# A two-layer diffusion step on one core: when weight tiles are split, and where modulation steps stand in a tile

## The chip, the core and the metric

The kernel runs on one core of a Trainium2 chip. The metric is the device time of one launch in microseconds. The engines named below are TensorE (PE, with its weight loads as PEld), VectorE (DVE), ScalarE (ACT), GpSimd (POOL) and SyncE (SP, which here only issues transfers). Each engine runs its own instructions strictly in the order of the program, and waits at an instruction until what it needs is there.

## What is computed

Two groups of rows (512 rows of a sample, 128 of a prompt, 640 in all) go through the same two layers. Cut to what matters:

```python
sh1, sc1, ga1, sh2, sc2, ga2 = split(silu(c) @ w_ada[l] + b_ada[l], 6)   # modulation
h = rmsnorm(x) * (1 + sc1) + sh1
z = h @ w_in[l]              # q, k, v | gq, gk, gv, gate, gate ranks
o_na  = attention(q, k, v)   # sample: window and cached keys; prompt: all keys
o_gla = gated_linear_attention(gq, gk, gv, forget gates), both directions
x = x + ga1 * (concat(o_na, rmsnorm(o_gla) * silu(gate)) @ w_o[l])
x = x + ga2 * (relu((rmsnorm(x) * (1 + sc2) + sh2) @ w_up[l]) ** 2 @ w_down[l])
```

All matrices are 1024 wide, the hidden layer of the MLP 4096. Everything is to be had at the accuracy of fp32.

## The kernel before

Activations lie transposed: 8 blocks of 128 features by 640 rows. A weight tile is 128x1024 (512 KB). A **split** makes two tiles of it: `wh`, a rounded copy (ACT), and `wl`, what the rounding lost (POOL, or DVE at the start of the program). A block of activations is split likewise, and a product is the sum of three: `wh` by the high part, `wh` by the low part, `wl` by the high part (`mm3`). A tile of the projection (`proj`) takes eight such groups, one for each block `kc`, six matrix products each, and then an evacuation from PSUM.

Weights come through three stages in `prefetch`: a transfer from SP's queue into a raw buffer `wr` (three of them), the split into a pair `wh`, `wl` (three pairs), and the use. `used`, called at the end of a tile, sets its pair free and calls `prefetch`, which at once writes down the split of a further tile, ahead of the evacuation of the tile that has just ended. So two tiles are ready when a tile begins, and the third is split while that tile runs.

The **modulation steps** (`ada_step`) work out `silu(c) @ w_ada` for all of layer 1 and most of layer 0, a 128x1024 tile of `w_ada` at a time, on DVE: two `scalar_tensor_tensor` instructions, one for each condition (`cbc`), each with an accumulated sum. In layer 0's attention half there is one step for each of the projection's tiles 6 to 23, and some more in the output projection. There `adab` is 1, and the raw tile of a step takes one of the same three `wr` buffers; in the MLP half (`adab` is 2) the steps have buffers of their own (`ar`). With `adab` 1 a step is written down after the evacuation of its tile.

Between the weight products PE takes the small products of attention, written as generators (`gla_pair`, `gv_task`, `qk_task`, `na_unit`) which a planner (`Drv`, with times estimated by `Est`) slips in between the groups of a tile. PE's order is fixed by that. The order on the other engines is set by a list scheduler, by priority and estimated time: `high_priority(offset=650)` in `prefetch` puts splits and transfers ahead of what was written before them. A dependency of class `NoSync` binds that order alone: no wait is put into the program for it.

Names in the traces: `ks`, `ksT` are decayed keys and their transposed copy, `ST` (in layer 1 `cbc`) the states, `ex` decay factors, `PN`, `tot` their sums, `A`, `Dg` the score blocks, `row` an activation block (here also a head's output), `sqo` its square, `gt`, `V`, `gv` values, `sq`, `sqh`, `sql` squares for the QK-norm, `gg` the output gate, `junk` a place for results that nobody reads. Every instruction carries line 197, that of a helper that records it, so groups go by names.

Of the kernel before, what the change touches and what calls it, by code (L numbers as in the profile page):

```python
# [211 lines left out]
class Kern:  # L212
# [13 lines left out]
    def run(self):  # L226
# [43 lines left out]
        self.wprep = self.wused = self.nada = 0  # L270
        self.adap, self.adab = None, 1
        self.wx = None
        self.raw, self.hl, self.over = {}, {}, set()
        self.rot, self.nacc = False, 0
        with self.pool("start") as sp, self.pool("norm_s", 2) as npl:
# [142 lines left out]
        for _ in range(self.steps_at(*key)):  # L418
            self.ada_step(*self.steps.pop(0))

    def prefetch(self, ahead=650):
        nc = self.nc
        with self.tc.high_priority(offset=ahead):
            go = True
            while go:
                go = False
                i = self.nld
                if i < min(len(self.units), self.npos + self.DEPTH, self.ldmax):
# [26 lines left out]
                    elif len(self.raw) + (self.nada if self.adab == 1 else 0) < self.NRAW:  # L455
# [2 lines left out]
                        self.raw[i] = t  # L458
                        self.nld += 1
                        go = True  # L460
                if self.raw and self.wprep - self.wused < (self.NHL if self.wx is None else self.NHL + 1):
                    j = min(self.raw)
                    wx = self.wx is not None and self.wprep == self.NHL
                    t = self.raw.pop(j)
                    if wx:
                        h, lo = (self.wx.tile([128, 1024], F32R, name=n) for n in ("wxh", "wxl"))
                    else:
                        h = self.wp.tile([128, 1024], F32R, name="wh", tag="wh", bufs=self.NHL)
                        lo = self.wp.tile([128, 1024], F32R, name="wl", tag="wl", bufs=self.NHL)
                    self.est.ready[t.name] = max(self.est.ready[t.name], self.dv.t)  # L470
                    nc.scalar.activation(out=h, in_=t, func=AF.Copy)
                    if self.wx is not None:
                        nc.vector.tensor_tensor(out=lo, in0=t, in1=h.bitcast(F32), op=ALU.subtract)
                    elif self.units[j] in self.units[max(0, j - 4):j] + self.units[j + 1:j + 5]:

                        nc.vector.tensor_tensor(out=lo[:, :448], in0=t[:, :448], in1=h[:, :448].bitcast(F32), op=ALU.subtract)
                        nc.gpsimd.tensor_tensor(out=lo[:, 448:], in0=t[:, 448:], in1=h[:, 448:].bitcast(F32), op=ALU.subtract)
                    else:
                        nc.gpsimd.tensor_tensor(out=lo, in0=t, in1=h.bitcast(F32), op=ALU.subtract)
                    self.hl[j] = (h, lo)  # L480
                    self.wprep += 1
                    go = True

    def unit(self, *key):
        i = self.ntake
# [15 lines left out]
    def ada_step(self, l, v, kc):  # L501


        nc = self.nc
        ui, t = self.unit("ada", l, v, kc)
        junk = self.junk()
        for r in range(2):
            i = nc.vector.scalar_tensor_tensor(out=junk if r == 0 else t, in0=t, scalar=1.0, in1=self.cbc[:, r], op0=ALU.mult,
                                           op1=ALU.mult, accum_out=self.mod[l][:, v, kc, r:r + 1])
            if self.adab == 1:  # L510

                self.tc.add_manual_dep(i.ins, self.lastmm.ins.name, mybir.DependencyInfo(
                    mybir.DependencyClass.NoSync, mybir.DependencyReason.DATA), reason="order")
        if kc == KC - 1:
            b0 = PC_BADA + 48 * l + 8 * v
            m = self.mod[l][:, v]
            nc.vector.tensor_tensor(out=m, in0=m, in1=self.pc[:, b0:b0 + KC, None].to_broadcast([128, KC, 2]), op=ALU.add)
        self.used(ui)
# [77 lines left out]
    def proj(self, key, evac):  # L596

        n = TX if self.lateh else T
        ui, w = self.unit(*key)
        wh, wl = (t.rearrange("p (k m) -> p k m", k=KC) for t in w)  # L600
        ps, nsm = self.acc_any(n=n)
        for kc in range(KC):
            self.mm3(ps, wh[:, kc], wl[:, kc], *self.h[kc], kc == 0, kc == KC - 1)
            if kc == 0 and self.adab > 1:
                self.ada_at(*key)
            if kc < KC - 1:
                yield
        self.used(ui)
        with self.tc.high_priority(offset=self.EVP):
            evac(ps[1])  # L610
        self.acc_done(ps, nsm)
        if self.adab == 1:
            self.ada_at(*key)
        yield

    def first_steps(self, keys):
# [250 lines left out]
    def layer(self, l):  # L867
# [11 lines left out]
        with self.pool(f"att{l}", reuse_waits="tile") as ap:  # L879
# [7 lines left out]
            with self.pool(f"gla{l}", reuse_waits="tile") as gp:  # L887
# [22 lines left out]
                    self.filler(self.z_tile(l, z_evac))  # L910
                else:
                    self.filler(self.first_b(l, [z_evac] + [lambda segs, i=i: self.gla_rope(l, 0, i, segs) for i in range(2)]))
                for h in range(2 if l == 0 else 0, 4):
                    dv.take("gt")
                    self.filler(self.proj(nxt(), lambda ps: self.start(self.gv_task(h, ps))))
# [17 lines left out]
            with self.pool(f"na{l}", reuse_waits="tile") as np_:  # L933
# [13 lines left out]
                for h in range(4):  # L947
                    hh, hl = self.pair_rows(ra, h)
                    nc.scalar.activation(out=hh, in_=self.gg[h], func=AF.Copy)
                    nc.gpsimd.tensor_tensor(out=hl, in0=self.gg[h], in1=hh.bitcast(F32), op=ALU.subtract)  # L950
                    self.aT[4 + h] = (hh, hl)
                x = [self.row(rb, kc, F32) for kc in range(KC)]
                for j in range(4):
                    for kc in range(2 * j, 2 * j + 2):
# [779 lines left out]
```

## Time and profile before

| | before |
|---|---|
| three runs, us | 1740.12, 1748.31, 1747.23 (median 1747.23) |
| profiled execution, its own time, us | 1745.39 |
| its span, us | 1743.6 |
| PE busy | 1653.4 us, 95% of the span |
| DVE, ACT, POOL busy | 62%, 40%, 36% |
| mean granted clock of TensorE | 0.979 |
| read from memory | 170.36 MB, 102 GB/s over the span |

The program has a start (0 to 60 us), the attention half of layer 0 (60 to 460: gated linear attention up to 260, then neighbourhood attention), the MLP half of layer 0 (460 to 880), the attention half of layer 1 (880 to 1300) and the MLP half of layer 1 (to the end). The page's line of 40 slices shows PE at 9 tenths or more in the MLP halves, and at 7 to 9 in the attention halves. A time in brackets in the rows is how long the engine stood idle ahead of the instruction, and the name behind it is what ended that. The granted clock is 1.00 at 2.4 GHz and 0.50 at 1.2 GHz.

### The profile page before, as it was taken

The numbers are of one execution on the slowest core, as the hardware profiler recorded it, in microseconds if no ns is written. First come the engines' busy times: TensorE is split into PE (matmuls) and PEld (weight loads), VectorE is DVE, ScalarE is ACT, GpSimd is POOL, SyncE is SP. The second block draws the span as 40 slices with busy tenths as digits, with TensorE's granted clock in tenths as the row PEclk, the third lists the DMA queues.
The fourth block names the chain that finished last, engine by engine and source line by source line (L and its number), as shares of the span: only waits on it lengthen the run. The fifth ranks groups of instructions, "written<-read, shape, count | busy, mean of one in ns | idle before, by whom it ended". The sixth has DMA issues, their size and how long they took to land. (4 is left out here: it accounts for less than half of the span.)

```text
span 1743.6 us, 32610 instructions
## 1 busy us (share of the span) xinstructions
PE 1653.4 (95%) x13712; PEld 1575.1 (90%) x13712; DVE 1076.4 (62%) x1971; ACT 703.3 (40%) x1142; POOL 626.7 (36%) x266
## 2 busy tenths in 40 slices
PE   7988788989999999999989899999999999999999
PEld 6977677779999999999988788888999999999998
DVE  5686767788797788777677737586662222222322
ACT  3535335543543233322344445466454223332330
POOL 1234432113334444444345536313233333333331
PEclk9998899999999999999999989999999999999999
DMA  9121233233354454445241111323222222222221
GB/s 369 45 65 64 92 105 119 77 110 121 121 181 139 157 166 134 144 147 169 76 168 51 51 43 57 91 69 94 70 65 84 73 73 73 74 83 74 73 73 73
DMA packets 61345, 179.28 MB, mean 103 GB/s; under 512 B 6928, under 2 KB 17808, under 8 KB 61200
## 3 DMA queue, kind: packets, MB, share of 16 engines
q1 hardware_dynamic: 45360, 159.76, 27.4%
q10 hardware_dynamic: 15840, 17.45, 3.2%
q8 instruction: 108, 1.77, 0.4%
q14 instruction: 37, 0.30, 0.1%
HBM read 170.36 MB, written 6.82 MB: 102 GB/s over the span
## 5 line engine op out<-in xcount | busy, mean ns | idle before, releaser
L197 POOL TENSOR_TENSOR wl<-wr,wh 128x1024 fp32r<-128x1024 f32 (+1 forms) x188 | 490.1, 2608 | 906.0 <-ACT wh L197 856.5
L197 PE MATMUL ps_mm<-row,wh 128*128 128x256 f32 (+1 forms) x2416 | 485.8, 322 | 7.9 <-DVE row L197 3.7
L197 ACT ACTIVATE wh<-wr 128x1024 fp32r<-128x1024 f32 x195 | 206.3, 1058 | 627.7 <-PE ps_sm L197 400.7
L197 PEld LDWEIGHTS ps_mm<-row,wh 128*128 128x128 f32 x2416 | 399.7, 193 | 30.3 <-issue 18.7
L197 PE MATMUL ps_mm<-row,wl 128*128 128x256 f32 (+2 forms) x1208 | 282.7, 313 | 0.5 <-DVE wl L197 0.5
L197 PEld LDWEIGHTS ps_mm<-row,wl 128*128 128x128 f32 x1208 | 224.8, 192 | 0.9 <-DVE wl L197 0.7
L197 DVE SCALAR_TENSOR_TENSOR row<-ps_sm,mod,row 128x256 f32<-128x256 f32 (+1 forms) x216 | 81.8, 432 | 97.0 <-PE ps_sm L197 97.0
L197 DVE SCALAR_TENSOR_TENSOR row<-ps_mm,mod,row 128x128 f32<-128x128 f32 (+2 forms) x180 | 89.4, 536 | 79.2 <-PE ps_mm L197 79.0
L197 DVE SCALAR_TENSOR_TENSOR ar<-ar,cbc 128x1024 f32<-128x1024 f32 x56 | 122.7, 2199 | 0.8
L197 ACT ACTIVATE r<-r 128x640 f32<-128x640 f32 (+2 forms) x192 | 112.3, 617 | 18.6 <-DVE r L197 15.1
L197 PE MATMUL ps_sm<-uh,wh 128*128 128x256 f32 (+1 forms) x512 | 119.2, 309 | 0.0
L197 PE MATMUL ps_mm<-uh,wh 128*128 128x256 f32 (+1 forms) x512 | 119.2, 309 | 0.0
L197 PE MATMUL ps_mm<-ul,wh 128*128 128x256 f32 (+1 forms) x512 | 119.0, 309 | 0.0
L197 PE MATMUL ps_sm<-uh,wl 128*128 128x256 f32 (+1 forms) x512 | 118.9, 309 | 0.0
L197 PE MATMUL ps_sm<-ul,wh 128*128 128x256 f32 (+1 forms) x512 | 118.9, 309 | 0.0
L197 PE MATMUL ps_mm<-uh,wl 128*128 128x256 f32 (+1 forms) x512 | 118.9, 309 | 0.0
L197 PE MATMUL ps_sm<-row,wh 128*128 128x256 f32 (+1 forms) x624 | 118.6, 309 | 0.0
L197 DVE TENSOR_TENSOR ul<-r,uh 128x640 fp32r<-128x640 f32 x64 | 55.2, 862 | 84.5 <-ACT r L197 84.4
L197 DVE TENSOR_TENSOR r<-ps_mm,rstd 128x642 f32<-128x642 f32 x34 | 28.1, 827 | 123.7 <-PE ps_mm L197 123.7
L197 PEld LDWEIGHTS ps_sm<-row,wh 128*128 128x128 f32 x624 | 103.0, 189 | 0.0
L197 PE MATMUL ps_mm<-m,wh 128*128 128x256 f32 (+1 forms) x544 | 102.3, 310 | 0.0
L197 DVE SCALAR_TENSOR_TENSOR r<-ar,cbc 128x1024 bf16<-128x1024 f32 x56 | 93.6, 1689 | 0.0
(203 smaller groups left out, 2947.1 us busy)
## 6 DMA issues: line engine op xcount, KB each, us to landing
wr<-w_dn SPq DMA_DIRECT2D x68, 512.0 KB, 3.5
wr<-w_up SPq DMA_DIRECT2D x64, 512.0 KB, 3.5
ar<-w_ada SPq DMA_DIRECT2D x56, 512.0 KB, 3.7
wr<-w_in SPq DMA_DIRECT2D x48, 512.0 KB, 3.5
wr<-w_ada SPq DMA_DIRECT2D x24, 512.0 KB, 3.5
wa<-w_ada SPq DMA_DIRECT2D x16, 512.0 KB, 10.2
wr<-w_o SPq DMA_DIRECT2D x16, 512.0 KB, 3.5
tab<-bias ACTq DMA_DIRECT2D x32, 96.0 KB, 2.2
```

Source lines behind the costliest of these rows:

```text
L197: r = f(*args, **kw)
```

## The change

There are three edits. A flag `late` is on in both layers from the latent projection on until the output gates have been split; while it is on, the call of `prefetch` at a tile's end holds back the last of the three pairs, and a new call within the next tile (`more=1`) splits it: after group 5 in layer 0, after group 1 in layer 1. A split on ACT is ordered behind the product written last (`behind`, as the modulation steps were), while `late` is on and in all of layer 0's attention half. A modulation step with `adab` 1 is written down after group 3 of its tile instead of after the evacuation. No instruction is added or taken away.

```diff
-    def prefetch(self, ahead=650):
+    def prefetch(self, ahead=650, more=0):
...
-                if self.raw and self.wprep - self.wused < (self.NHL if self.wx is None else self.NHL + 1):
+                if self.raw and self.wprep - self.wused < (self.NHL if self.wx is None else self.NHL + 1) - (self.late and not more):
...
-                    nc.scalar.activation(out=h, in_=t, func=AF.Copy)
+                    self.behind(nc.scalar.activation(out=h, in_=t, func=AF.Copy))
...
+    def behind(self, i):
+
+        if self.late or self.adap is not None and self.adab == 1:
+            self.tc.add_manual_dep(i.ins, self.lastmm.ins.name, mybir.DependencyInfo(
+                mybir.DependencyClass.NoSync, mybir.DependencyReason.DATA), reason="order")
...
-            if self.adab == 1:
-
-                self.tc.add_manual_dep(i.ins, self.lastmm.ins.name, mybir.DependencyInfo(
-                    mybir.DependencyClass.NoSync, mybir.DependencyReason.DATA), reason="order")
+            self.behind(i)
...
-            if kc == 0 and self.adab > 1:
+            if kc == (0 if self.adab > 1 else 3):
                 self.ada_at(*key)
+            if key[0] == "in" and kc == (5 if self.adap is not None else 1):
+                self.prefetch(more=1)
...
-        if self.adab == 1:
-            self.ada_at(*key)
...
+                self.late = True
                 for h in range(2 if l == 0 else 0, 4):
...
+                self.late = False
                 x = [self.row(rb, kc, F32) for kc in range(KC)]
```

What this does to the order is shown at three places, all in layer 0. The first is ACT, where the outputs of two heads of the first pair (`row_1`, `row_2`) are copied out of PSUM, each in a part of 512 and one of 128 columns.

```order
 L197 DMA ST<-state_fwd 128x128
-L197 ACTIVATE row_1_1738<-ps_sm 128x512
-L197 ACTIVATE wh<-wr 128x1024
-L197 ACTIVATE row_1_1738<-ps_sm 128x128
-L197 ACTIVATE row_2_1741<-ps_sm 128x512
-L197 ACTIVATE row_2_1741<-ps_sm 128x128
+L197 ACTIVATE row_1_1732<-ps_sm 128x512
+L197 ACTIVATE row_1_1732<-ps_sm 128x128
+L197 ACTIVATE row_2_1735<-ps_sm 128x512
+L197 ACTIVATE row_2_1735<-ps_sm 128x128
 L197 DMA ST<-state_bwd 128x128
```

The split that stood between the two parts of `row_1` now stands twelve activations later, behind work for the second pair's gates.

The second place is ACT again, some 35 us later, where the decayed keys of the second pair are copied (`ksT`). Before:

```order
L197 ACTIVATE gg_760<-ps_mm,pc 128x640
L197 ACTIVATE tmp<-ps_mm 128x640
L197 ACTIVATE tmp<-tmp 128x640 x2
L197 ACTIVATE wh<-wr 128x1024
L197 ACTIVATE ksT<-ps_sm 128x512 x2
L197 DMA new_sf<-ST 128x128
L197 ACTIVATE wh<-wr 128x1024
L197 ACTIVATE gt<-ps_mm 128x512
```

After:

```order
L197 ACTIVATE gg_760<-ps_mm,pc 128x640
L197 ACTIVATE tmp<-ps_mm 128x640
L197 ACTIVATE tmp<-tmp 128x640 x2
L197 ACTIVATE ksT<-ps_sm 128x512
L197 ACTIVATE wh<-wr 128x1024
L197 ACTIVATE ksT<-ps_sm 128x512
L197 DMA new_sf<-ST 128x128
L197 ACTIVATE gt<-ps_mm 128x512
```

The split ahead of the first `ksT` is gone from there (it stands earlier now, between two `ex`), and that of the tile after it stands between the two `ksT`.

The third place is DVE between these two, where the gates of the second pair begin (`tmp<-ps_sm,pc`, the running sum into `PN`). The rows with `cbc` are the two instructions of a modulation step.

```order
-L197 SCALAR_TENSOR_TENSOR junk,mod_107<-wr,cbc 128x1024
-L197 SCALAR_TENSOR_TENSOR wr,mod_107<-wr,cbc 128x1024
 L197 TENSOR_SCALAR tmp<-ps_sm,pc 128x256
 L197 TENSOR_SCALAR tmp<-ps_sm,pc 128x384
+L197 SCALAR_TENSOR_TENSOR junk,mod_107<-wr,cbc 128x1024
 L197 SCALAR_TENSOR_TENSOR PN<-tmp 128x128 x5
-L197 TENSOR_TENSOR row_1_1738<-row_1_1738,tmp 128x640
+L197 TENSOR_TENSOR row_1_1732<-row_1_1732,tmp 128x640
 L197 COPY tot<-PN 128x5
+L197 SCALAR_TENSOR_TENSOR wr,mod_107<-wr,cbc 128x1024
```

The step that was ahead of the gates (that of tile 9) has gone further ahead, and the step of tile 10 has moved in among them; it stood behind the four `ex` that follow.

## Rows read from the trace of the kernel before

**Rows 1.** By stage: us, PE, PEld, DVE, ACT, POOL busy, clock, DMA share, GB/s.

```profile
60.00:300.00 240.00, 203.84 (x2426) 183.20 (x2424) 181.88 (x300) 107.05 (x177) 84.53 (x35) 0.92 0.27 86
300.00:460.00 160.00, 146.62 (x1072) 129.51 (x1073) 131.25 (x317) 75.28 (x157) 38.58 (x16) 0.96 0.32 100
460.00:880.00 420.00, 420.00 (x2864) 420.00 (x2864) 324.49 (x455) 143.57 (x191) 176.03 (x60) 1.00 0.44 145
880.00:1300.00 420.00, 392.88 (x3879) 359.58 (x3878) 285.11 (x586) 210.26 (x383) 167.40 (x78) 0.98 0.24 76
```

**Rows 2.** Splits on ACT, 60 to 460 us: durations, what ended idle time.

```profile
L197 ACT ACTIVATE wh<-wr x31: 1040/1057/1062, 59.6 to 453.4; 128x1024 fp32r<-128x1024 f32 x31
...
  DMA wr<-w_in: 30.5, 10
```

**Rows 3.** Timeline, first place (start us, us, engine, instruction, idle before it).

```profile
144.53 0.58 ACT L197 ACTIVATE row<-ps_sm 128x512 f32<-128x512 f32 x1
149.59 1.06 ACT L197 ACTIVATE wh<-wr 128x1024 fp32r<-128x1024 f32 x1 [4.47 <-DMA wr<-w_in]
154.38 2.50 PE L197 MATMUL ps_mm<-sqo,ones 128*128 128x256 f32 x4 [5.41 <-POOL sqo L197]
```

**Rows 4.** Timeline, second place.

```profile
174.50 3.96 DVE L197 SCALAR_TENSOR_TENSOR wr<-wr,cbc 128x1024 f32<-128x1024 f32 x1
...
173.41 3.96 POOL L197 TENSOR_TENSOR ex<-ex,qk 128x1280 f32<-128x1280 f32 x1 [2.07 <-ACT ex L197]
...
178.49 0.33 SPq L197 DMA_DIRECT2D wr<-w_in  x1
...
181.87 1.06 ACT L197 ACTIVATE wh<-wr 128x1024 fp32r<-128x1024 f32 x1 [5.09 <-DMA wr<-w_in]
...
183.47 1.98 PE L197 MATMUL ps_sm<-gv,ksT 128*64 128x128 f32 x16 [7.16 <-ACT ksT L197]
```

**Rows 5.** Timeline, third place: a modulation step ahead of `V`.

```profile
191.61 3.42 DVE L197 SCALAR_TENSOR_TENSOR wr<-wr,cbc 128x1024 f32<-128x1024 f32 x1
...
197.36 0.78 PE L197 MATMUL ps_sm<-ex 64*64 64x64 f32 x32 [2.32 <-DVE V L197]
```

**Rows 6.** Timeline, fourth place: the outputs of the second pair.

```profile
241.30 1.06 ACT L197 ACTIVATE wh<-wr 128x1024 fp32r<-128x1024 f32 x1 [7.43 <-DMA wr<-w_in]
...
246.12 1.86 PE L197 MATMUL ps_mm<-sqo,ones 128*128 128x256 f32 x4 [1.92 <-POOL sqo L197]
```

**Rows 7.** Timeline, fifth place: a modulation step ahead of `sql`.

```profile
272.03 3.27 DVE L197 SCALAR_TENSOR_TENSOR wr<-wr,cbc 128x1024 f32<-128x1024 f32 x1
...
276.10 0.56 PE L197 MATMUL ps_mm<-sql,blk_r 128*128 128x256 f32 x2 [1.62 <-DVE sql L197]
```

**Rows 8.** Stretches behind these five waits, columns as in rows 1.

```profile
154.40:158.00 3.60, 3.60 (x10) 2.80 (x10) 0.00 (x0) 1.02 (x2) 1.14 (x1) 0.50 0.36 130
183.50:188.80 5.30, 5.30 (x30) 4.89 (x31) 1.74 (x5) 0.51 (x1) 3.02 (x2) 0.50 0.47 150
197.40:203.40 6.00, 5.73 (x95) 5.37 (x98) 2.41 (x6) 2.22 (x2) 2.37 (x2) 0.72 0.19 68
246.10:253.60 7.50, 6.50 (x18) 4.54 (x19) 1.29 (x2) 3.06 (x4) 2.72 (x2) 0.55 0.21 74
277.50:281.00 3.50, 3.50 (x13) 2.68 (x12) 3.46 (x16) 3.22 (x7) 0.00 (x0) 0.51 0.46 159
```

**Rows 9.** Groups by form, 60 to 460 us: count, busy us, mean ns, idle before.

```profile
L197 DVE SCALAR_TENSOR_TENSOR wr<-wr,cbc 128x1024 f32<-128x1024 f32 x24 | 41.3, 1720 | 0.6
L197 DVE SCALAR_TENSOR_TENSOR junk<-wr,cbc 128x1024 bf16<-128x1024 f32 x24 | 32.2, 1344 | 0.1
...
L197 POOL TENSOR_TENSOR wl<-wr,wh 128x1024 fp32r<-128x1024 f32 x27 | 68.3, 2530 | 199.1 <-ACT wh L197 189.4 <-PE ps_sm L197 9.7
```

**Rows 10.** Timeline: the score blocks of the second pair, layer 0.

```profile
231.57 3.71 DVE L197 COPY_PREDICATED A<-masks,Dg 32x320 f32<-32x320 int32 x4
```

**Rows 11.** Timeline, layer 1: a value tile behind a split.

```profile
962.35 0.76 PE L197 MATMUL ps_sm<-ident,gt 128*128 128x128 f32 x5 [1.17 <-ACT gt L197]
```

More of the change, by code (lines that the diff above doesn't have):

```diff
@@ L951, in layer @@
                     self.aT[4 + h] = (hh, hl)
+                self.late = False
                 x = [self.row(rb, kc, F32) for kc in range(KC)]
```

## The prediction, made before the changed kernel ran

> **What bounds the kernel now.** I read the busy times by stage first. From 460 to 880 us, the MLP half of layer 0, PE is busy all the time at a clock of 1.00 [rows 1], so no wait is left there for a change of order to take away. The change acts on the attention halves, and there PE does wait: 240 less 203.84 and 160 less 146.62 make 49.5 us of idle time in layer 0, 420 less 392.88 makes 27.1 us in layer 1 [rows 1]. No other engine is full in these stages; the fullest is DVE, with 181.88 of 240 us. So the halves are bound by chains that go from PE through DVE, ACT or POOL and back. The granted clock tells of a second cost: 0.92 and 0.96 in layer 0 [rows 1], which means stretches at 1.2 GHz behind the longer waits. At the most, all idle time and all lost clock of layer 0 could come back: 49.5 us, and 0.08 of 240 plus 0.04 of 160, which is 25.6 us.
>
> Next I asked who holds up ACT. Of the 31 splits from 60 to 460 us, ten begin only when a transfer of `w_in` has landed, and ACT stands idle 30.5 us for them [rows 2]. A split takes 1.06 us; the wait in front of it is what counts, since whatever stands behind it on ACT waits too. The trace shows two places where that reaches PE. At 144.53 ACT copies the first part of a head's output, then stands 4.47 us at a split, and PE waits 5.41 us for the square of that output [rows 3]. At 181.87 ACT has stood 5.09 us at a split, the copy `ksT` is behind it, and PE waits 7.16 us [rows 4]. The second has its root on DVE: the raw buffer for that transfer was still read by a modulation step until 174.50 plus 3.96, 178.46 us, and SP issues the transfer at 178.49 [rows 4]. So late steps hold transfers, transfers hold splits, splits hold ACT, and ACT holds PE.
>
> **The change part by part.** No instruction is added, so everything is a matter of what waits where. All sums are made against the profiled execution's 1745.4 us, which is 1.8 us under the median of the three runs; as a ratio the forecast holds for either.
>
> *First place.* In the new order both outputs are copied before the split. The stretch from the copy's end, 145.11, to the split's end, 150.65, goes from their path: 5.54 us, and that covers the wait of 5.41 us [rows 3]. Behind the wait PE ran 3.60 us at 0.50 [rows 8], which at full clock is half of that, 1.8 us. Gain 7.2 us.
>
> *Second place.* The step of tile 10 has moved up in front of the running sums, where DVE had stood waiting for ACT, so its buffer is free well before 178 us and the split of tile 13 finds its data. The first `ksT` has no split in front. But two splits stand earlier in the same chain on ACT (2.1 us), POOL now takes a gate's product ahead of the keys, and the step itself is in front of the sums, so the keys come later against PE than the first place alone would have them. I take 3 us of the 7.16 as left. Gain 4.2 us, and of the 5.30 us at 0.50 [rows 8], worth 2.65 us, I take 2.0: 6.2 us. Bounds: nothing, if the new work eats it, and 9.8 us.
>
> *Third place.* `V` stands behind a step's product of 3.42 us on DVE, and PE waits 2.32 us for it [rows 5]. In the new order that step comes after `V`. Behind it are 6.00 us at a mean of 0.72 [rows 8]: 3.4 us of them at half clock, a loss of 1.7. Gain up to 4.0; I take 3.0, since the factor product `ex` in front of `V` still waits for ACT.
>
> *Fourth place.* ACT stands 7.43 us at a split in front of the second pair's outputs, and PE waits 1.92 us for the square [rows 6]. With earlier steps the data is there, and POOL squares before it takes up the next `wl`. The stretch behind it has 6.50 us of PE's work in 7.50 at 0.55 [rows 8], some 5.8 us at half clock, a loss of 2.9. Gain up to 4.8; I take 4.0.
>
> *Fifth place.* A step's product of 3.27 us stands ahead of `sql`, and PE waits 1.62 us [rows 7]; the step is gone from there. With 3.50 us at 0.51 [rows 8], worth 1.7, it is 3.3 at most. The small products of neighbourhood attention are interleaved anew from there on, so I take half, 1.7.
>
> *Layer 1.* There are no steps here. At 962.35 PE waits 1.17 us for a value tile whose copy stood behind a split [rows 11]; with the split in the next tile the copy goes first, and 1.06 us come back. I count two such places, 2.0 us; bounds nothing and 4.
>
> *What it costs.* Before the score blocks of the second pair a step now stands that stood behind them. They took DVE from 231.57 for 3.71 us [rows 10]. A step's mean is 1.72 plus 1.34, 3.1 us [rows 9]; how much of that falls into a gap no row tells, and I take half on PE's path, 1.5 us. The first pair sees the same shift, but an earlier step has left its chain: 1.0 us. Together 2.5 us; bounds nothing and, with both steps in full, 6.2.
>
> *Neighbourhood attention from 300 us on.* The planner slips the products in at other groups, and which wait comes of it no row tells. All waits there are 13.4 us [rows 1]. I take nothing, and 6 us either way for the range.
>
> *Steps and splits at the same time.* The two modulation products are two-input reads on DVE, and `wl` is one on POOL. At 174.50 DVE's product began while POOL worked until 173.41 plus 3.96, 177.37, and ended 1.09 us after that [rows 4]: it had been blocked, and then ran. The rule for this is in the Trainium skill, page "SBUF — State Buffer", section "SBUF: two separate sides": the port pair that DVE and POOL share is an exclusive lock, which the one that starts first holds for its whole instruction. By that rule, a trace row agrees, and it speaks against this change, since steps and splits both move into the middle of a tile; that is the second rival.
>
> The sum: 7.2 + 6.2 + 3.0 + 4.0 + 1.7 + 2.0 - 2.5 is 21.6 us, and 1745.4 less 21.6 is 1723.8, say 1724 us.
>
> **The rivals.**
>
> *Late weights (slower).* A split had nearly two tiles' time, and has less now. A tile is 48 products, so 2864 of them in 420 us [rows 1] are 59.7 tiles of 7.04 us. Behind group 5 there are two groups (1.8 us) and a whole tile, 8.8 us, until the weights are used; the split takes 1.06 us on ACT [rows 2] and a mean of 2.53 on POOL [rows 9], so 5.2 us are left. A split behind an instruction at which ACT stands 7.43 us, the longest such wait in my rows [rows 6], is 2.2 us late, and with half clock behind it PE loses about 4 us. From six such tiles the gain is gone; with ten of the 40 tiles concerned it is 1724 plus 40, 1764 us. Against it: the ten waits that hold ACT are for transfers, which come sooner now, and inserted products stretch most tiles. In layer 1 the split is behind group 1, with 3.5 us more. Chance 0.10.
>
> *DVE takes half of it back.* The steps stand in the middle of a tile, in front of work that PE waits for, and meet `wl` on POOL. If three or four more of the 24 steps than I counted end in PE's path by their whole length of 3.1 us, 11 us go, and the time is 1735. Told by the blocking in rows 4: a second product with a whole `wl` of 2.53 us [rows 9] in front and 1.09 us of its own is 1.9 us over its mean, 24 of them 46 us, and with a quarter of that in PE's path it is 1735 too. That is what the rule of the Trainium skill's page "SBUF — State Buffer" would make of it. For it: DVE is the fullest engine behind PE, and two of the five places are steps ahead of what PE waited for. Against it: DVE had 58 us free of 240 [rows 1]. Chance 0.17.
>
> *It moves nothing.* The new dependency puts no wait into the program, so a reordered ACT could stand just as long at other instructions: 1745 us. The order printed above speaks against it, as the splits did change place. Chance 0.05.
>
> **How the numbers follow.** My forecast has 0.68, with a range of its own from 1712 to 1736. Half a per cent, about what a measurement of this kernel can tell from no change, is 8.7 us, so faster means under 1736.7. That holds nearly all of the forecast (0.66) and half of the second rival (0.09): 0.75. The same: the rest of these two (0.10) and the third rival's bulk (0.04), 0.14. Slower: the first rival and a rest, 0.11. The range from 1713 to 1743 leaves out the first and third rival and the forecast's outer end, some 0.2.
>
> **What would show it.** In the new profile the wait of PE for `sqo` at the first place is under 1 us and that for `ksT` under 4; splits on ACT from 60 to 460 us wait for `w_in` less than 10 us in all, and SP issues the transfer of tile 13 some 15 us earlier against PE. The clock from 60 to 300 us is 0.96 or more, and PE's idle time there falls from 36 to about 20 us. Layer 1's half shrinks by 1 to 4 us, and the MLP halves don't change by 1 us. I am wrong if PE waits for `wl` or `wh` at the start of tiles (the first rival), if DVE from 60 to 300 us is as full per us as PE (the second), or if neighbourhood attention in layer 0 grows by over 6 us.

## The result, and the profile after

The changed kernel takes 1756.79 us in the median (1750.78 to 1761.23), the kernel before beside it 1747.4 us. The ratio is 1.0059 with a 95% interval of 1.0041 to 1.0076: slower by 7 to 13 us, where 1724 was forecast and 1743 was the upper end of the range. The profiled execution of the changed kernel, which its rows below are from, was the shortest of its executions: its span is 1749.0 us, 5.4 over that of before. The other 4 us or so of the medians' difference are not placed here; in its other executions the mean granted clock was 0.971 to 0.975 against 0.979 in this one.

By stage, columns as in [rows 1]:

```profile
60.00:300.00 240.00, 205.50 (x2434) 186.75 (x2434) 190.97 (x302) 106.27 (x176) 93.08 (x34) 0.91 0.26 85
300.00:460.00 160.00, 150.25 (x1140) 135.13 (x1137) 127.50 (x320) 80.74 (x166) 41.65 (x19) 1.00 0.36 112
460.00:880.00 420.00, 418.63 (x2867) 418.31 (x2866) 330.32 (x465) 142.33 (x190) 176.97 (x62) 1.00 0.44 145
880.00:1300.00 420.00, 382.43 (x3757) 347.88 (x3758) 282.26 (x573) 205.05 (x374) 156.35 (x74) 0.96 0.22 72
```

From 60 to 300 us PE's idle time is 34.5 us, where before it was 36.2, and the clock is no better; DVE and POOL are 9 us fuller each. From 880 to 1300 PE is idle 37.6 us, 10 more than before, at a lower clock.

These windows are cut by the clock on the wall, and a kernel that is ahead has other work in them. So I count PE's weight products (48 a tile, 9168 in all, those that read `wh` or `wl`), take from the timeline the start of the first one of a tile, and compare lengths between the same products. These starts are, in us:

```
tile               4      16      32     100     112     124
before          80.3   255.0   461.5   967.6  1115.7  1265.0
whole change    78.9   254.4   449.5   955.3  1110.1  1270.4
```

In the kernel before, gated linear attention of layer 0 (tiles 4 to 16) takes 174.7 us, neighbourhood attention and output of layer 0 (16 to 32) 206.5, gated linear attention of layer 1 (100 to 112) 148.1 and neighbourhood attention of layer 1 (112 to 124) 149.4. In the changed kernel these four are **+0.7, -11.3, +6.7 and +11.0 us**; what lies between and behind them moves by 0.3 us, and the start by -1.4. The sum is the 5.4 us between the two spans. So this is no "nothing happened": two large changes of opposite sign, a gain that is missing, and a loss where nothing was expected.

In the first stage the forecast waits did go. PE's wait for `sqo` [rows 3] and that for `V` [rows 5] are not in the list any more; these are, among others, from the waits of PE between 60 and 300 us (total, times, longest):

```profile
PE ps_sm L197 <- DVE A L197: 5.2, 1, 5.2
PE ps_sm L197 <- POOL ks L197: 4.9, 1, 4.9
PE ps_sm L197 <- ACT ksT L197: 4.9, 1, 4.9
...
PE ps_sm L197 <- DVE Dg L197: 3.7, 1, 3.7
```

The first of them, in the timeline of the changed kernel, is a step in the middle of a tile that meets POOL twice:

```profile
133.31 1.55 POOL L197 TENSOR_TENSOR gg<-gg,tmp 128x640 f32<-128x640 f32 x1 [4.94 <-ACT tmp L197]
133.47 2.48 DVE L197 SCALAR_TENSOR_TENSOR junk<-wr,cbc 128x1024 bf16<-128x1024 f32 x1
...
135.31 2.87 POOL L197 TENSOR_TENSOR wl<-wr,wh 128x1024 fp32r<-128x1024 f32 x1 [0.45 <-ACT wh L197]
135.99 3.28 DVE L197 SCALAR_TENSOR_TENSOR wr<-wr,cbc 128x1024 f32<-128x1024 f32 x1
...
139.79 3.29 DVE L197 COPY_PREDICATED A<-masks,Dg 32x320 f32<-32x320 int32 x4
...
143.13 1.23 PE L197 MATMUL ps_sm<-A,gv 128*128 128x128 f32 x4 [5.17 <-DVE A L197]
```

A step's product takes 1.22 us when nothing is in its way. Here the first starts at 133.47 while POOL works to 134.86, and ends at 135.95, 1.09 us after POOL's end; the second starts at 135.99 while POOL is in `wl` until 138.18, and ends at 139.27, again 1.09 after it. The two take 5.76 us instead of 2.4, the score masks stand behind them, and PE waits 5.17 us. That is the blocking that was seen at one place in [rows 4]. In the attention half of layer 0 it holds 12 of the changed kernel's 48 step products, and each of the 12 ends 1.08 or 1.09 us after an instruction of POOL. It goes the other way as well: `wl`, 2.35 us at the least in this stretch, begins at 135.31 while the first product runs, and ends 2.23 us after that product. The Trainium skill, page "SBUF — State Buffer", section "SBUF: two separate sides", says that the port pair which DVE and POOL share is locked by the one that starts first for its whole instruction, and that the other is fully blocked; this trace agrees.

From 60 to 270 us 10 of the changed kernel's 26 step products are held in this way, where in the kernel before it was 5 of 24 (and in e3, with the steps at the tile's end, 5 of 26).

### The profile page after: what moved, and what is told of

The parts are those of the page before. It is cut to its first block, busy times and chain, and to the rows that moved or that the text cites. A ratio compares the mean times of both kernels' runs of the same rounds, so it can differ in the third digit from the quotient of the medians.

```text
span 1749.0 us, 32563 instructions
## 1 busy us (share of the span) xinstructions
PE 1653.1 (95%) x13712; PEld 1577.0 (90%) x13712; DVE 1085.4 (62%) x1971; ACT 702.4 (40%) x1142; POOL 628.0 (36%) x266
## 4 chain that ended last, share of the span: by engine, by line
PE 60%; DVE 10%; ACT 3%; issue 2%; POOL 1%; DMA 0%; ACTq 0%; DVEq 0%; POOLq 0%
PE ps_mm L197 32%; PE ps_sm L197 28%; DVE ex L197 2%; DVE row L197 2%; DVE sqa L197 1%; ACT wh L197 1%; DVE tmp L197 1%; DVE m L197 1%; DVE y L197 1%; DVE s L197 1%; DVE PN L197 0%; ACT ex L197 0%; ACT tmp L197 0%; DMA wr<-w_o 0%; PE ps_ss L197 0%
## 5 line engine op out<-in xcount | busy, mean ns | idle before, releaser
L197 ACT ACTIVATE r<-r 128x640 f32<-128x640 f32 (+2 forms) x192 | 112.3, 617 | 18.6 <-DVE r L197 15.1
L197 PEld LDWEIGHTS ps_sm<-ul,wh 128*128 128x128 f32 x512 | 93.5, 188 | 0.0
```

The lines of the kernel that those rows point to most:

```text
L197: r = f(*args, **kw)
```

## The experiments

Each of the twelve was timed beside the kernel before on one chip, not all of them on the same one, so ratios are to be compared. What they say by stage is in one table behind them; "stages" means the four above.

**One layer at a time (e1, e4).** In e1 the hold-back is off in layer 1, and every engine's order there is that of before; e4 moves the splits of layer 1 alone.

```
-                self.late = True
+                self.late = l == 0
```

> The whole change in layer 0; in layer 1 splits stay as in the kernel before (the hold-back is off there), and every engine's order in layer 1 is that of before. Theory A (the late splits of layer 1 cost the time: against the same weight products the changed kernel loses 6.7 us in the gated linear attention of layer 1 and 11.0 us in its neighbourhood attention, and gains 10.6 us in layer 0): about 12 us under the kernel before, 1733 to 1738 us, with layer 1's half at 392 to 394 us of busy PE. Theory B (the profiled execution misleads, the loss is spread over the program as a lower clock): 1750 to 1757 us, as the whole change.

> Only the splits of layer 1 move; layer 0 is that of before. Theory A: 14 to 20 us slower than before, 1761 to 1767 us. Theory B: within 4 us of before.

Measured: e1 1735.04 us, ratio 0.9941 (0.9920 to 0.9962); e4 1760.69 us, ratio 1.0089 (1.0068 to 1.0109). Theory A stands: the change gains some 10 us in layer 0 and loses some 15 in layer 1, and theory B is out.

**One part at a time in layer 0 (e2, e3).** e2 has only the steps in the middle of a tile; e3 has only the splits, with these lines put back:

```
+        if self.adab == 1:
+            self.ada_at(*key)
         yield
```

> Only the modulation steps move into the middle of a tile; splits stand as in the kernel before, in both layers. Theory C (steps in the middle of a tile meet the split's product on POOL and take back in the gated linear attention what the splits give): slower than before, 4 to 10 us of it between tiles 4 and 16 of layer 0. Theory D (steps are what frees raw buffers and so what ends ACT's waits for transfers; they carry layer 0's gain): 8 to 14 us faster than before, and the waits of splits for input weights on ACT fall from 30.5 to about 17 us.

> Only the splits of layer 0 move behind a product of the next tile; steps stay at the tile's end, layer 1 is that of before. Theory C (steps take back what splits give): 8 to 14 us faster than before, with the gain in the gated linear attention, where PE no longer waits 5.41 us for the square of the head's output. Theory D (steps carry the gain): within 4 us of before, since transfers still come late.

Measured: e2 1737.49 us, 0.9947 (0.9926 to 0.9967); e3 1735.10 us, 0.9942 (0.9923 to 0.9960). Each part alone gives about what both together give in e1. They do it in different stages: e3 gains 12.8 us in gated linear attention and loses 2.7 in the neighbourhood stage, e2 gains 3.4 and 5.5. In e2 the splits' waits for input weights fall from 30.5 us [rows 2] to 18.1, as theory D had it. Theory C had steps alone slower in gated linear attention; they are not, though in e2 the planner made an order of PE of its own, so this is not the steps' place alone. What costs is both parts together: -12.8 with the splits alone, -5.0 (e1) and +0.7 (the whole change) with steps as well. In these three PE's order of this stage is the same, product by product; e1 and the whole change also have the same code there, so the 5.7 us between them are the spread of single executions.

**Where the steps stand (e7).** Splits of layer 0 as in the change; steps at the tile's end until neighbourhood attention begins, and from there in the middle.

```
+        mid = self.mid
...
-            if kc == (0 if self.adab > 1 else 3):
+            if kc == 0 and self.adab > 1 or kc == 3 and self.adab == 1 and mid:
```

> Layer 1 as before; in layer 0 the splits of the change, with the modulation steps at the end of a tile during gated linear attention and in the middle of one from the first tile of neighbourhood attention on. Theory C (steps in the middle of a tile cost in gated linear attention and gain in neighbourhood attention; splits the other way round): the two gains add, 11 to 14 us by tile 16 and 5 to 10 us more by tile 26, so 1722 to 1730 us. If the gains don't add (transfers are early with either edit, and each edit alone has most of it): 1732 to 1738 us.

Measured: 1727.56 us, 0.9898 (0.9883 to 0.9913). The two gains add, 13.1 and 5.1 us; this is faster than either kernel. (Its profiled execution was the fastest of its four, and 4.6 us of its lead lie in layer 1, where it has the code of before.)

**The steps' time (e9).** The results of the steps are of 64 columns only.

```
+        n = 64 if self.adap is not None and self.adab == 1 and not self.mid else D
...
+            i = nc.vector.scalar_tensor_tensor(out=(junk if r == 0 else t)[:, :n], in0=t[:, :n], scalar=1.0, in1=self.cbc[:, r, :n],
```

> The changed kernel with PE's order held to its own by replay; the modulation steps of the gated linear attention of layer 0 read 64 of their 1024 columns (so their results are of a part of the sum), which takes some 1.7 us off each of 26 products while buffers, transfers and places stay. Theory C (in the middle of a tile the steps' time is what takes the splits' gain back): from tile 4 to tile 16 it is 9 to 14 us faster than before, where the whole change was 0.7 us slower, and about 1743 to 1748 us in all. If it is not the steps' time: the gated linear attention stays within 4 us of before, and the whole is 1752 to 1758 us.

Measured: 1738.36 us, 0.9956 (0.9938 to 0.9975), with 16.5 us gained in gated linear attention: more than expected, the direction of theory C. With shorter steps other DVE instructions changed places too, so the size is not of the steps' time alone. Nor were 1.7 us taken off each of 26 products: 22 were shortened from 60 to 270 us, to means of 0.88 and 0.95 us, though the shortest took 0.21. At the place shown above they are held until POOL is done, like the long ones, and PE waits for the score masks as it did there:

```profile
129.96 1.49 DVE L197 SCALAR_TENSOR_TENSOR junk<-wr,cbc 128x64 bf16<-128x64 f32 x1
...
131.49 2.27 DVE L197 SCALAR_TENSOR_TENSOR wr<-wr,cbc 128x64 f32<-128x64 f32 x1
...
137.65 1.22 PE L197 MATMUL ps_sm<-A,gv 128*128 128x128 f32 x4 [5.39 <-DVE A L197]
```

Of the 3.8 us that the two take here some 0.4 are their own; what stands in the way at this place is the blocking, and e9's gain lies elsewhere.

**Places and PE's order apart (e5, e6).** The planner puts the small products among the weight products by its own estimate of when operands are ready, and a split that is noted later changes that estimate. For this pair I wrote out which tasks the planner had stepped behind each group, and replayed that list in the other kernel. The other engines' orders still come from the list scheduler, and follow:

```
+    def go(self, *_):
+        i = self.n
+        self.n += 1
+        for s in self.plan[i]:
+            next(self.gens[s], None)
+
+    take = until = drain = go
```

> All of the change, in both layers, but PE's instructions in exactly the order of the kernel before (the planner's decisions of that kernel are written into the program as a list and replayed). So splits and steps stand where the change puts them, and no small product moves against the weight products. Theory E (layer 1 loses because the planner, with the split noted later, puts small products one group earlier, ahead of their operands): layer 1 is within -4 to +3 us of before, where the change with its own order lost 17.7, and the waits for POOL's ks (2.73 us) and DVE's pT (3.95 us) are gone; in all 1732 to 1742 us. Theory F (the split itself is in the way on ACT and POOL in the middle of a tile): layer 1 still loses 12 to 18 us, 1745 to 1757 us in all. Of layer 0's neighbourhood attention it tells as well whether its gain of some 10 us comes of the steps (it stays) or of the new order of its products (it goes).

> The other half of that pair: splits and steps as in the kernel before, PE's instructions in exactly the order of the changed kernel, replayed. Theory E: layer 1 loses 10 to 20 us though no split has moved. Theory F: layer 1 within 4 us of before. In layer 0's neighbourhood attention a gain of some 10 us without any moved step would say that the new order of products made it.

Measured: e5 1744.15 us, 0.9987 (0.9978 to 0.9997); e6 1740.08 us, 0.9960 (0.9947 to 0.9972). Neither theory has layer 1 to itself, and neither one's sum for it came in e5 (+4.1 us). In its neighbourhood attention the new order alone, with no split moved, loses 9.0 us, and the moved splits with the old order lose nothing (-0.3): theory E. In its gated linear attention it is the other way round: moved splits +4.4, new order -7.3: theory F. PE's waits say the same: in e5 that for `ks` stays, 2.7 us, and of those for `pT` 0.5 us are left; in e6 there is none for `ks` and 0.2 us for `pT`. And in layer 0 the gain of the neighbourhood stage goes with the new order, -10.8 without a moved step against -2.2 with all moved and the old order.

**POOL (e8, e10).** Theory F needed a place. In layer 1 of the changed kernel a moved split puts `wl` ahead of POOL's `ks`, with PE waiting 2.73 us for it; and in neighbourhood attention `wl` and a gate's product hold DVE's `qT`:

```profile
1038.94 2.58 POOL L197 TENSOR_TENSOR wl<-wr,wh 128x1024 fp32r<-128x1024 f32 x1 [6.72 <-ACT wh L197]
...
1041.48 2.82 POOL L197 TENSOR_TENSOR gg<-gg,tmp 128x640 f32<-128x640 f32 x1
...
1044.26 2.88 POOL L197 TENSOR_TENSOR ks<-ks,qk 128x1280 f32<-128x1280 f32 x1
...
1047.20 1.11 PE L197 MATMUL ps_sm<-ident,ks 128*128 128x128 f32 x4 [2.73 <-POOL ks L197]
...
1197.98 2.40 POOL L197 TENSOR_TENSOR wl<-wr,wh 128x1024 fp32r<-128x1024 f32 x1 [1.38 <-ACT wh L197]
...
1198.56 4.37 DVE L197 SCALAR_TENSOR_TENSOR qT<-raw,gq,rs 128x512 f32<-128x512 f32 x2 [0.53 <-ACT rs L197]
...
1206.22 1.28 DVE L197 COPY pT<-ps_sm 128x512 f32<-128x512 f32 x2
...
1206.95 0.43 PE L197 MATMUL ps_sm<-kT,qT 64*128 64x192 f32 x1 [3.95 <-DVE pT L197]
```

So e8 keeps all of the change and PE's order, and puts `wl` on DVE while splits are held back; e10 does the same to the kernel before, over the same stretch, with PE's order held and nothing else edited.

```
-                    if self.wx is not None:
+                    if self.wx is not None or self.late:
                         nc.vector.tensor_tensor(out=lo, in0=t, in1=h.bitcast(F32), op=ALU.subtract)
```

> The changed kernel with PE's order held to its own by replay; while splits are held back, the product wl of a split runs on DVE (1.22 us there in the rows of the start, against a mean of 2.46 to 2.88 on POOL), so nothing of the moved splits stands on POOL. Theory G (the moved splits cost by POOL: wl stands ahead of POOL's ks, for which PE then waits 2.73 us, and blocks DVE's products, as qT, 4.37 us for two where the other trace has 1.41, with PE waiting 3.95 us for the copy pT behind them): these two waits go, layer 1 loses 0 to 8 us against before and not 17.7, and in layer 0 the first step products of 60 to 270 us come down from a mean of 1.82 to 1.3 to 1.5 us; in all 1735 to 1747 us. Theory H (DVE has no room; what counts is how much stands on it): the same or slower than the whole change, 1755 to 1775 us.

> The kernel before, with PE's order held to its own by replay, in which wl of the splits runs on DVE over the same stretches of the program as in the run e8 (from the tile of z to the end of the attention's products); nothing is moved. Theory G (POOL's wl costs because the change puts it in the middle of a tile): splits at the tile's end harm little on POOL, so this gains less than 10 us on the kernel before, 1736 to 1750 us, and the gain of e8 on the change, 34 us, needs both edits. Rival (wl is better on DVE anywhere, and the change adds nothing to it): 1715 to 1728 us, as e8.

Measured: e8 1722.47 us, 0.9869 (0.9850 to 0.9887); e10 1716.94 us, 0.9831 (0.9804 to 0.9859). In e8 the same pair of `qT`, in the same order of PE, takes 1.41 us, and the products behind the copies `pT` start without a wait:

```profile
1170.86 1.41 DVE L197 SCALAR_TENSOR_TENSOR qT<-raw,gq,rs 128x512 f32<-128x512 f32 x2
...
1173.18 1.28 DVE L197 COPY pT<-ps_sm 128x512 f32<-128x512 f32 x2
...
1174.21 0.60 PE L197 MATMUL ps_sm<-kT,qT 64*128 64x192 f32 x4
```

Theory G is right on the whole change, some 33 us better by the two ratios with `wl` off POOL, and theory H is out. Of G's signs, the two waits go and layer 1 loses 2.5 us; the step products from 60 to 270 us come down from 1.82 and 1.91 us to 1.69 and 1.41, the first ones less than G had it. And one reading falls: neighbourhood attention of layer 1 is still 9.8 us longer than before with the waits for `qT` and `pT` gone, so they were not what it costs there.

e10 refutes the rest of G: the kernel before gains 29 us by the same edit with no split and no step moved by it. What the change had to fight was in the kernel before already. Two places show how. The fourth is the plainer: in both kernels ACT makes the split first and then copies the outputs. In the kernel before, the first square can start only when `wl` is off POOL, and PE waits 1.92 us [rows 6]:

```profile
242.26 1.40 ACT L197 ACTIVATE row<-ps_sm 128x512 f32<-128x512 f32 x4
242.49 2.37 POOL L197 TENSOR_TENSOR wl<-wr,wh 128x1024 fp32r<-128x1024 f32 x1 [9.18 <-ACT wh L197]
...
244.82 2.46 POOL L197 TENSOR_TENSOR sqo<-row 128x640 f32<-128x640 f32 x2
```

In e10 POOL is free and squares as the copies end:

```profile
228.00 1.40 ACT L197 ACTIVATE row<-ps_sm 128x512 f32<-128x512 f32 x4
...
229.37 2.47 POOL L197 TENSOR_TENSOR sqo<-row 128x640 f32<-128x640 f32 x2 [21.02 <-PE ps_sm L197]
...
230.68 1.34 PE L197 MATMUL ps_mm<-sqo,ones 128*128 128x256 f32 x4 [0.54 <-POOL sqo L197]
```

At the first place two things come together. In the kernel before:

```profile
141.94 2.78 POOL L197 TENSOR_TENSOR wl<-wr,wh 128x1024 fp32r<-128x1024 f32 x1 [6.11 <-ACT wh L197]
...
144.75 0.33 SPq L197 DMA_DIRECT2D wr<-w_ada  x1
145.17 0.38 SPq L197 DMA_DIRECT2D wr<-w_in  x1
...
150.77 2.35 POOL L197 TENSOR_TENSOR wl<-wr,wh 128x1024 fp32r<-128x1024 f32 x1 [4.49 <-ACT wh L197]
...
153.08 2.46 POOL L197 TENSOR_TENSOR sqo<-row 128x640 f32<-128x640 f32 x2
```

and in e10, up to PE's product of the square:

```profile
139.31 1.22 DVE L197 TENSOR_TENSOR wl<-wr,wh 128x1024 fp32r<-128x1024 f32 x1
...
140.56 0.33 SPq L197 DMA_DIRECT2D wr<-w_in  x1
...
142.14 0.76 ACT L197 ACTIVATE row<-ps_sm 128x512 f32<-128x512 f32 x2
...
142.76 2.47 POOL L197 TENSOR_TENSOR sqo<-row 128x640 f32<-128x640 f32 x2
...
145.35 1.06 ACT L197 ACTIVATE wh<-wr 128x1024 fp32r<-128x1024 f32 x1 [2.45 <-DMA wr<-w_in]
145.78 0.48 PE L197 MATMUL ps_mm<-sqo,ones 128*128 128x256 f32 x1
```

Before, `wl` reads a raw buffer until 144.72; the transfer into that buffer goes out at 144.75, and the one of `w_in` behind it on SP's queue at 145.17. The split at 149.59 stands ahead of the last copies, the next `wl` ahead of the squares, and PE waits 5.41 us [rows 3]. On DVE `wl` takes 1.22 us, the transfer of `w_in` goes out as it ends, and PE finds `sqo` there. But the copies now stand ahead of the split on ACT: no edit put them there, the list scheduler did, and it is the order that the change gives to this place. So part of what e10 gains here is ACT's order and not POOL's time; how much, no run shows.

**Both findings put together (e11, e12).** e11 is e8 with PE's old order in layer 1; e12 has the steps of gated linear attention back at the tile's end as well.

> The run e8 (all of the change, wl on DVE while splits are held back), with PE's order of the changed kernel in layer 0 and that of the kernel before in layer 1. In e8 the neighbourhood attention of layer 1 is still some 10 us longer than before; by theory E, for this stage (there it is the planner's new order of small products that costs, with e6 at +9.0, e5 at -0.3 and the whole change at +11.0 us), it comes back to within 3 us of before, and the whole is 1708 to 1716 us. If the late split itself costs there: the stage stays 8 us or more over before, 1719 to 1726 us.

> As the run e11 (all of the change, wl on DVE while splits are held back, PE's order of the changed kernel in layer 0 and of the kernel before in layer 1), but with the modulation steps at the tile's end in the gated linear attention of layer 0 and in the middle of a tile only from its neighbourhood attention on. If steps in the middle of a tile cost there even when no wl stands on POOL (e11 gained 12.4 us from tile 4 to 16, the kernel before with wl on DVE 17.3): that stage gains 16 to 21 us and the whole is 1704 to 1710 us. If they cost only by meeting POOL's wl: the stage stays at 10 to 14 us and the whole at 1710 to 1716 us.

Measured: e11 1712.78 us, 0.9818 (0.9795 to 0.9842); e12 1713.68 us, 0.9811 (0.9792 to 0.9829). With the old order neighbourhood attention of layer 1 comes back to -1.8 us, as expected. Moving the steps no longer matters (-12.4 and -13.8): without POOL's `wl` in the middle of a tile they cost nothing that can be seen. Together with the splits alone (e3, e7) against both parts (e1, the whole change) this says that the loss in gated linear attention needs both, steps in the middle and `wl` on POOL. Whether the change adds anything to e10 is not settled; the intervals overlap.

Lengths of the stages against the kernel before, us, one profiled execution each (GLA is gated linear attention, NA neighbourhood attention):

```
                                      layer 0 GLA   layer 0 NA   layer 1 GLA   layer 1 NA
whole change                              +0.7         -11.3         +6.7         +11.0
e1  layer 0 alone                         -5.0          -9.4         -2.9          +1.5
e2  steps alone                           -3.4          -5.5         +0.2          +1.7
e3  splits of layer 0 alone              -12.8          +2.7         -2.1          +0.2
e4  splits of layer 1 alone               -2.9          +3.2         +6.8         +11.0
e5  change, PE's order of before          -1.4          -2.2         +4.4          -0.3
e6  before, PE's order of the change      -0.4         -10.8         -7.3          +9.0
e7  splits layer 0, steps in NA          -13.1          -5.1         -4.6           0.0
e8  change, wl on DVE                    -13.4         -14.3         -7.3          +9.8
e9  change, short steps                  -16.5          -7.7         +5.5         +13.8
e10 before, wl on DVE                    -17.3          -2.7         -6.6          -2.1
e11 e8, old order in layer 1             -12.4         -15.1         -5.4          -1.8
e12 e11, steps in NA                     -13.8         -10.4         -5.1          -1.8
```

How sure these are: e4 has the code and order of before in layer 0, e1, e2, e3 and e7 have it in layer 1, and they show -2.9 and +3.2, and -4.6 to +1.7. The whole change, e1, e7 and e9 have the same code and the same order of PE in neighbourhood attention of layer 0, and show -5.1 to -11.3.

Against that, neighbourhood attention of layer 1 parts cleanly by PE's order: +9.0 to +13.8 us in the five runs with the change's, -2.1 to +1.7 in the eight others, all with before's. PE's idle time in the stage parts with it, 7.4 to 11.0 us against 2.0 to 3.4. In layer 0 the lengths part less clearly: -5.1 to -15.1 us in the eight runs with the change's order, -2.7 to +3.2 in the four with before's (that kernel itself, e4, e5 and e10). The idle time of PE is 10.4 to 15.6 us in the eight and 17.4 to 18.5 in the four. e2 and e3 have orders of their own there; e3 has about three quarters of its small products where the change has them, and gains nothing. So which part of the new order helps in layer 0 is not shown.

## Why the prediction was wrong

**What bounds the kernel: half right.** The chain from late steps to transfers, splits, ACT and PE is there, and shortening it with the splits alone gave 12.8 and 13.1 us in gated linear attention (e3, e7), against the 17.9 that the first four places less the cost were to bring. But POOL's part of it was read too short. `wl`, a mean of 2.53 us [rows 9], stands ahead of POOL's own work, blocks DVE's products and reads the raw buffer as well, and I used that row only for the rivals. e10 shows what the three are worth together: 17.3 us in this stage with no split and no step moved by an edit, some of it by ACT's new order at the first place.

**The five places.** First, third and fourth: the waits went, as forecast. Second: 4.88 us are left for `ksT`, where 3 were forecast, with a new wait of 4.90 for `ks` in front of it. The waits for `A`, `ks` and `Dg` took their place, and the stage gained nothing. The fifth lies where PE's new order decides, and can't be told by itself.

**The step that failed first: "What it costs".** I took 2.5 us, with 6.2 as the bound, for two steps at their mean of 3.1 us. The runs say 8 to 14 us: -12.8 and -13.1 without the steps' move, -5.0 and +0.7 with it, with the same order of PE. The mean was the wrong price, since a step's length depends on where it stands: 3.73 us in the changed kernel and 3.08 in e3. From 60 to 270 us, the groups of the changed kernel and then of e3 (count, busy us, mean ns):

```profile
L197 DVE SCALAR_TENSOR_TENSOR wr<-wr,cbc 128x1024 f32<-128x1024 f32 x13 | 24.8, 1909 | 0.3
L197 DVE SCALAR_TENSOR_TENSOR junk<-wr,cbc 128x1024 bf16<-128x1024 f32 x13 | 23.7, 1822 | 0.1
...
L197 POOL TENSOR_TENSOR wl<-wr,wh 128x1024 fp32r<-128x1024 f32 x12 | 34.5, 2877 | 20.3 <-ACT wh L197 20.3
```

```profile
L197 DVE SCALAR_TENSOR_TENSOR wr<-wr,cbc 128x1024 f32<-128x1024 f32 x13 | 22.0, 1693 | 0.3
L197 DVE SCALAR_TENSOR_TENSOR junk<-wr,cbc 128x1024 bf16<-128x1024 f32 x13 | 18.0, 1385 | 0.1
```

That is the second rival, which had 0.17 and was to take half back: the mechanism was the right one, and it took all of this stage's gain (in e1, with the same code, more than half of it). My argument against it, that DVE had 58 us free of 240, was no argument, since a product that is blocked stands in a chain however empty its engine is on average.

**The step that failed worst: "Layer 1".** Forecast -2.0 us with bounds of 0 and -4; measured +17.7. I thought of what goes away behind a moved split, and not of what it now stands in front of. In gated linear attention that is POOL's `ks` and DVE's products (+4.4 to +6.8 with `wl` on POOL, -5.1 to -7.3 with `wl` on DVE). In neighbourhood attention it is the planner's answer to the change: with the split noted later the evacuation looks earlier to it, some 60% of the small products there stand one or two groups (of six weight products) earlier, and with that order the stage is 9 to 14 us longer wherever the splits stand.

**The term that was mis-sized: "Neighbourhood attention from 300 us on".** Nothing, with 6 us either way; measured -11.3 in layer 0, which includes the fifth place. That no row tells which waits come of a new order was right; that the answer is small was not. The new order alone went with -10.8 us in one layer and +9.0 in the other (e6), so the range should have held both.

**The rivals.** Late weights did not come: in the profile of the changed kernel PE waits 0.5 us for `wl` in all of its products with the rows.

```profile
L197 PE MATMUL ps_mm<-row,wl 128*128 128x256 f32 (+2 forms) x1208 | 283.0, 313 | 0.5 <-DVE wl L197 0.5
```

So the slower outcome came, but by another way than the rival for it. "It moves nothing" is wrong by stage, though the total looks like it.

**The signs named beforehand.** Right: `sqo` at the first place under 1 us; the MLP half of layer 0 unchanged; and of the transfers, tile 13's goes out at 166.70 instead of 178.49 us [rows 4], 12 us sooner where some 15 were named. Wrong: `ksT`; the clock and PE's idle time from 60 to 300 us; layer 1; and the splits' waits, which fell by half and not to under 10 us:

```profile
L197 ACT ACTIVATE wh<-wr x32: 1038/1051/1086, 60.0 to 456.9; 128x1024 fp32r<-128x1024 f32 x32
...
  DMA wr<-w_in: 16.6, 4
```

Of the three "I am wrong if", none came true as it was put: PE did not wait for weights, neighbourhood attention of layer 0 shrank, and DVE from 60 to 300 us is fuller by 9 us but, with 190.97 us, not as full as PE with 205.50. The second rival came all the same, so its sign was the wrong one: not how full DVE is, but how long its products stand.

**What stays open.** How much of POOL's `wl` costs by blocking DVE, how much by standing ahead of POOL's own work and how much by holding the raw buffer was not taken apart; the rows show one or two places of each. In e10 the list scheduler gave ACT another order at the first place, and no run holds the orders of ACT, DVE and POOL while `wl` moves.

## What to carry to other kernels

Before you move an instruction, price what it will stand in front of, on its engine and on any engine that it can block; its mean in the old place is not its price in the new one. When a planner sets the order of the bound engine from estimates, hold that order fixed in one run, or a change of a few instructions is measured together with a reshuffle that can be worth as much with either sign; and look at what the list scheduler does to the other engines in that run. And a two-input product on POOL that sits in several waits at once deserves the first experiment: on DVE `wl` took 1.22 us here where nothing blocked it, for means of 2.46 to 2.88 on POOL in the attention halves of the changed kernel (the Trainium skill, page "GPSIMD Engine Reference", section "4.1 Engine selection", says of two-input elementwise work that POOL is about twice as slow and VectorE is to be used; this case agrees), and that one edit was worth 29 us, with DVE the fullest engine behind PE.

## What the hardware showed that I had not expected

A blocked instruction is held until the other engine's instruction ends, however small it is itself. In the kernel before, a DVE sum of five columns, which else takes some 0.15 us, stood 2.37 us until POOL's `wl` ended at 1049.54:

```profile
1046.63 2.91 POOL L197 TENSOR_TENSOR wl<-wr,wh 128x1024 fp32r<-128x1024 f32 x1 [4.41 <-ACT wh L197]
...
1047.20 2.37 DVE L197 TENSOR_TENSOR tot<-tot,PN 128x5 f32<-128x5 f32 x1
```

And one-input work of DVE is drawn out in the same way: scaling 512 columns of `s` takes 0.49 us, and 1.57 and 1.59 at 1203.03 and 1204.70 in the changed kernel, while POOL was in the gates' products; each of the two ends some 0.28 us after one of POOL's three.

```profile
1201.12 4.89 POOL L197 TENSOR_TENSOR row<-gg,row 128x640 fp32r<-128x640 f32 x3 [0.75 <-ACT row L197]
...
1203.03 1.57 DVE L197 TENSOR_SCALAR s<-s,st 128x512 f32<-128x512 f32 x1
...
1204.70 1.59 DVE L197 TENSOR_SCALAR s<-s,st 128x512 f32<-128x512 f32 x1
```
